# Decoder trunk on one core: weights and inputs of three TensorE stages put at other addresses, and the narrow score products of four head pairs reordered

## The chip, the core and the metric

The kernel runs on one core of a Trainium2 chip. The metric is the device time of one execution in microseconds (us); lower is better. The kernel before takes 551.02 us (median of three runs: 679.29, 551.02 and 550.89 us). A core has TensorE (PE in the profile; its weight loads are shown apart as PEld), VectorE (DVE), ScalarE (ACT), GpSimd (POOL) and SyncE (SP), which here issues nearly all DMAs. On-chip memory (SBUF) is addressed by a partition, of which there are 128, and a byte offset within it. When this text says that a tile lies "at 256", it means its byte offset within a partition modulo 512.

## The reference

One decoder layer for 256 tokens of width 1024: a convolution branch and a sparse-attention branch side by side, a cross-attention into 256 memory tokens, and a gated feed-forward block. Cut to what matters:

```python
h = rms_norm(x, norm_mix_g)
(u_conv, q, kc, vc, ks, vs, kw, vw, g_heads, g_conv, g_attn) = split(h @ w_in)
conv_out = conv_module(u_conv, ...)                  # gated, depthwise over time, layer norm, pointwise
nsa_out  = nsa_attention(q, kc, vc, ks, vs, kw, vw)  # compressed, selected and window branches
x = x + (sigmoid(g_conv) * conv_out + sigmoid(g_attn) * nsa_out) @ w_out

h = rms_norm(x, norm_x_g)
k, v = split(mem @ wkv)
s = einsum("bshd,bmhd->bhsm", h @ wq, k) / sqrt(256)
o = einsum("bhsm,bmhd->bshd", softmax(s), v)
x = x + o @ wo                                       # cross output

a, b = split(rms_norm(x, norm_ffn_g) @ ffn_in)
x = x + (silu(a) * b) @ ffn_out
return rms_norm(x, final_norm_g)
```

`ks` and `kw` are the keys of the selected and the window branch, `vs` and `vw` their values; 16 query heads share 4 groups of them. All arrays are float32. With 256 tokens, all four blocks of the selected branch are taken, so both branches see all earlier keys.

## The kernel before

**Products in three terms.** Each large product `W x` is formed from values split in two: a rounded copy (`..h`) and the remainder (`..l`). `split` (from L172) makes both for a half chunk of weights, 128 partitions by 4 blocks of 128 rows by 256 columns: ScalarE writes the copy (L184) and VectorE the remainder (L186). `rows` (L265 to L283) then issues three groups of 8 matmuls for a half chunk, each 128x128 by 256 columns: copy by copy, copy by remainder, remainder by copy. A chunk has two halves, so a chunk `ks`, `kw`, `gc0`, `xo0` and so on is 48 matmuls at L280. `x[..]` (the moving operand, or stream) and the weights each lie at one place modulo 512 throughout a group of 8. For `vs`, `vw` and the `v` chunks the roles are exchanged: the activations are loaded as weights and the weight tile is streamed.

**Where tiles lie.** The copies come from a ring `whi` of 5 buffers of 4096 bytes, the remainders from a ring `wlo` of 5. Large tiles share slots `L0` to `L14` and `LL` one after the other; a slot lies where its first tile was made, and it is as large as its largest tile. Added up in that order, L0 to L6, L9, LL, L10 and L14 start at 0 (modulo 512). L14 holds 8448 bytes, because of `kdl`, so L12, L11 and L13 start at 256. Behind L13 comes a filler tile `gap` of 320 bytes, and with it `whi` and `wlo` start at 64. So the usual pair is weights at 64, stream at 0 (`hh`, `hl`, `memh`, `meml`, `z`, `yh`, `yl`, `gh_1`, `gl_1` all lie at 0).

**Halves set apart.** `set_apart` (L195) puts one half chunk elsewhere: `k3_0` has its copy in L14 at 256 and its remainder in L10 at 448; `xq1_0` and `xo0_0` both have theirs in LL, at 256 and 448. The cross output's input `oxh` lies in L13, at 256, and `oxl` in L9, at 0 (L994). L11 holds `kvt`, then `sga`, then `pxh`; L13 holds `zins`, then `sgc`, then `oxh`; L14 holds, late in the program, `yl` and then `first_fo`, the first two half chunks of the feed-forward output weights, which are loaded long before use.

**Order.** The program is written as one sequence, and the framework's planner orders each engine's instructions when the program is built, by estimated times and the order in the text. On the chip each engine keeps that order and waits on semaphores. `in_line()` ties a matmul behind the one before it, so `ks` to `gc3`, the scores and the transposes stay in the written order on TensorE.

**Scores.** `scores(hp)` handles heads 2hp and 2hp+1 with queries in two halves. `later_half(hd)` is the second half of the queries against 512 key columns: two matmuls of 512 columns (L761, with `kdh` and then `kdl`). The first half of the queries needs 256 columns per head: two "narrow" matmuls each (L769). The order is wide (first head), narrow, narrow, wide (second head). VectorE then adds the bias and takes the minimum (L774 for the narrow results of both heads, then L780 for the wide ones). `scores(0)` stands before `ga3`, `scores(1)` in front of the second period, and so on through `between()`, which hands out the 8-matmul groups of `gc0` to `gc3` and `v0` to `v3` as filling.

**Cross output.** `cross_output(j)` (L1038) forms head j's output from `pxh`, `pxl` (both at 256) and `vxh`, `vxl` (both at 0, loaded as weights). `later_half(names, x)` below it runs `xo0` to `xo3` on `oxh`, `oxl`: the first halves of `xo0` to `xo2` fill in between the last softmax steps (L280), the second halves follow in one block of 72 matmuls (L1073), and `xo3` ends it with 48 (L280).

Of the kernel before, what the change touches and what calls it, by code (L numbers as in the profile page):

```python
# [10 lines left out]
F32R = mybir.dt.float32r  # L11
# [4 lines left out]
P = 128  # L16
D = 1024
S = 256
NB = D // P
# [79 lines left out]
def tile_hybrid_block(  # L99
# [15 lines left out]
    nc = tc.nc  # L115
    PSUM = bass.MemoryType.PSUM
    sb = ctx.enter_context(tc.tile_pool(name="sb", bufs=1))
# [4 lines left out]
    def long(name, slot, shape=(P, NB, S), dt=F32):  # L122

        return sb.tile(list(shape), dt, tag=f"L{slot}", name=name)

    def longs(names, slots, dt=F32R):
        return [long(n, i, dt=dt) for n, i in zip(names, slots)]
# [6 lines left out]
    def small(name, shape, dt=F32, tag=None, bufs=1):  # L134
        return sb.tile(shape, dt, tag=tag or name, name=name, bufs=bufs)

    def bank(name):

        four.append(0)
        if "s" in four[0] and len(four) % 2:  # L140
            return axp.tile([P, 2, S], F32, tag="s", name=name, bufs=2)
        return mmp.tile([P, 2, S], F32, tag="mm", name=name)
# [3 lines left out]
    def aux(name, shape, tag, bufs):  # L146
        return axp.tile(shape, F32, tag=tag, name=name, bufs=bufs)

    def f(ap):
        return ap.bitcast(F32)  # L150
# [20 lines left out]

    def split(w, shape, name):  # L172
        if name in apart:
            hi = apart[name]()[:, 64:].rearrange("p (k c) -> p k c", k=shape[1])
        else:
            hi = small(f"{name}h", shape, F32R, tag="whi", bufs=5)
        if name in apart:
            lo = aparts[name]().rearrange("p (k c) -> p k c", k=shape[1])
        else:
            lo = small(f"{name}l", shape, F32R, **places[1 - into_ffn(name)])  # L180

        n = 2 if name == "k1_0" else shape[1]
        with behind(*first.get(name, ())):
            copies = [nc.scalar.activation(hi[:, at:at + n], w[:, at:at + n], AF.Copy) for at in range(0, shape[1], n)]  # L184
            for at in range(0, shape[1], n):
                low = nc.vector.tensor_tensor(out=lo[:, at:at + n], in0=w[:, at:at + n], in1=f(hi[:, at:at + n]), op=ALU.subtract)  # L186
        splits[name] = copies[-1], low
        return hi, lo


    first, splits, apart = {}, {}, {}

    aparts = {}

    def set_apart(name, tag, low=None):  # L195

        pair = []

        def hi():
            pair.append(sb.tile([P, 1024 + 64 if low else 2 * 1024 + 112], F32R, tag=tag, name=f"{name}h"))  # L200
            return pair[0][:, 0:1024 + 64]

        def lo():
            if low:
                return sb.tile([P, 1024 + 112], F32R, tag=low, name=f"{name}l")[:, 112:]
            return pair[0][:, 1024 + 112:]

        apart[name], aparts[name] = hi, lo

    set_apart("k3_0", "L14", "L10")  # L210
    set_apart("xq1_0", "LL")
    set_apart("xo0_0", "LL")

    def behind(*marks):

        stack = ExitStack()
        for m in marks:
            stack.enter_context(tc.issue_after(m.ins))
        return stack
# [13 lines left out]
    def into_ffn(name):  # L233
        return name[0] == "f" and name[1] != "o"
# [9 lines left out]
    def halved(name, i):  # L244
        return split(raw(name, i), [P, 4, 256], f"{name}_{i}")
# [18 lines left out]
    last = []  # L264

    def in_line():
        return behind(*last)
# [17 lines left out]
    def sweep(*args, **kw):  # L285
        for _ in rows(*args, **kw):
            pass
# [94 lines left out]
    mem, h = (memh, meml), (hh, hl)  # L382
# [13 lines left out]
        ahead(name, slot)  # L396
    roots(0)

    small("gap", [P, 80])

    def kx(j):
        ps = gemm(f"k{j}", mem) if j else whole("k0", mem_t)
# [99 lines left out]
    with behind(loads["u6_1"]):  # L502
# [4 lines left out]
                     start=True, stop=True)  # L507
# [3 lines left out]
    for qb in range(2):  # L511
        for i, ns in enumerate(CGROUPS):
            n0, n1 = ns[0], ns[-1] + 1
            nc.tensor.matmul(cb_ps[:, qb, n0:n1].rearrange("p n h -> p (n h)"), lhsT=cbt[:, i, qb * P:qb * P + P],
                             rhs=relt[:, RT_CB + 16 * n0:RT_CB + 16 * n1], start=True, stop=True)
# [7 lines left out]
    def bias_of(hp):  # L523

        t = small(f"nb{hp}", [P, 2, S], tag="nb", bufs=2)
        for k in range(2):
            nc.sync.dma_start(t[:, k], bass.AP(tensor=row.tensor, offset=row.offset + 8 * 384 * (2 * hp + k) + P - 1,
                                               ap=[[384 - 16, 8], [-1, 16], [1, S]]))
        return t
# [180 lines left out]
    def qh(hd, qb):  # L710
        return qt[hd // 8][:, hd % 8, qb * P:qb * P + P]
# [34 lines left out]
    def heads_of(hp):  # L746
        return 2 * hp, 2 * hp + 1

    def scores(hp):

        g = hp // 2
        nbp = bias_of(hp)
        s0 = aux(f"s0_{hp}", [P, 2, 2, P], "s0", 1)
        p0 = small(f"p0_{hp}", [P, 2, 2, P], tag="p0", bufs=2)
        s1s, p1 = [], []

        def later_half(hd):
            s1 = aux(f"s1_{hd}", [P, 2, S], "s", 2)
            with in_line():
                for i, t in enumerate((kdh, kdl)):  # L760
                    mm = nc.tensor.matmul(s1, lhsT=qh(hd, 1), rhs=t[:, g].rearrange("p b t -> p (b t)"), start=i == 0, stop=i == 1)  # L761
            last[:] = [mm]
            s1s.append(s1)

        later_half(2 * hp)
        for k, hd in enumerate(heads_of(hp)):
            with in_line():
                for i, t in enumerate((kdh, kdl)):
                    mm = nc.tensor.matmul(s0[:, k], lhsT=qh(hd, 0), rhs=t[:, g, :, 0:P], start=i == 0, stop=i == 1)  # L769
        last[:] = [mm]  # L770
        later_half(2 * hp + 1)
        for k, hd in enumerate(heads_of(hp)):
            for br in range(2):
                red = nc.vector.tensor_tensor_reduce(out=p0[:, k, br], in0=s0[:, k, br], in1=nbp[:, k, P:S], scale=1.0, scalar=3e38,  # L774
                                                     op0=ALU.add, op1=ALU.min, accum_out=mins[:, hd, 0, br:br + 1])
        for k, hd in enumerate(heads_of(hp)):
            p1.append(small(f"p1_{hd}", [P, 2, S], tag="pr", bufs=4))
            for br in range(2):
                with behind(red):
                    low = nc.vector.tensor_tensor_reduce(out=p1[k][:, br], in0=s1s[k][:, br], in1=nbp[:, k], scale=1.0, scalar=3e38,  # L780
                                                   op0=ALU.add, op1=ALU.min, accum_out=mins[:, hd, 1, br:br + 1])
        mins_of.append(low)
        if hp == 1:
            first["gc2_1"] = red,
        return p0, p1
# [65 lines left out]

    mins_of = []
    p = [scores(0)]
    late = gate(3)
    with behind(mark):
# [28 lines left out]
    for hp, n in enumerate(PERIODS):  # L884
        if hp < 7:
            p.append(scores(hp + 1))
            with behind(*copies[-3:]):
                weights(hp + 1, *p[hp + 1])
        if hp == 2:
            pc_ps = aux("pc_ps", [P, 4, P], "pt", 2)  # L890
            with in_line():
                for qb in range(2):
                    for i in range(2):
                        mm = nc.tensor.transpose(pc_ps[:, 2 * i + qb], nsc[:, qb, 8 * i:8 * i + 8].rearrange("p h n -> p (h n)"), ident)
# [96 lines left out]

    r16 = rnorm(acc1, "2", 256.0)
    xmax, xneg, xsum = (small(n, [P, 4, 2]) for n in ("xmax", "xneg", "xsum"))
    oxh, oxl, pxh, pxl = longs(("oxh", "oxl", "pxh", "pxl"), (13, 9, 11, 12))  # L994
    queries = {}
    four[0] = ""

# [58 lines left out]
    def later_half(names, x):  # L1056

        pss = [bank(f"ps_{n}") if j < 2 else aux(f"ps_{n}", [P, 2, S], "s", 2) for j, n in enumerate(names)]
        parts = {}
        for n, ps in zip(names, pss):  # L1060
            for i in range(2):
                parts[n, i] = halved(n, i)
                if i == 0 or n == names[-1]:
                    with behind(*tail_mark) if n == names[0] else ExitStack():
                        sweep(ps, parts[n, i], x, i, line=False)
            if n == names[2]:
                for ks in ((0, 1), (2, 3)):
                    for m, qs in zip(names[:3], pss):
                        for row, (wi, xi) in enumerate(((0, 0), (0, 1), (1, 0))):
                            for b in range(2):  # L1070
                                cs = slice(b * P, b * P + P)
                                for k in ks:
                                    nc.tensor.matmul(qs[:, b], lhsT=parts[m, 1][wi][:, k, cs], rhs=x[xi][:, 4 + k], start=False,  # L1073
                                                     stop=k == 3 and row == 2 and b == 1)
                        if ks[1] == 3:
                            yield m, qs
        yield names[-1], pss[-1]
# [224 lines left out]
```

## Time and profile before

| | |
|---|---|
| runs | 679.29, 551.02, 550.89 us; median 551.02 |
| profiled execution | 551.26 us, of which the span from its first to its last instruction is 549.2 us |
| TensorE busy | 541.3 us (99%), 3886 matmuls |
| VectorE, ScalarE, GpSimd busy | 417.9 us (76%), 360.4 us (66%), 140.0 us (25%) |
| DMA queue that SP feeds | 95.86 MB, 52.3% of 16 engines' span |
| granted TensorE clock, mean | 0.999 |

A row of the chain of waits gives a start in us from the span's beginning, a length in us and what ran, with the number of instructions. A row of the timeline has the same first two columns, then engine, line, operation, output and inputs, the shape and the count. Matmuls overlap: the length of a timeline row includes the tail of its last matmul, so the distance of one row's start to the next one's start is the time that the group took from TensorE. Buffer and chunk numbers are left out of names, so `ks_0h` is the copy of a first half.

### The profile page before, as it was taken

What the parts mean: (1) busy time and instruction counts of PE and PEld (TensorE: products, weight loads), DVE (VectorE), ACT (ScalarE), POOL (GpSimd) and SP (SyncE); (2) the same over time, 40 slices, a digit from 0 to 9 for tenths busy, and PEclk for the clock granted to TensorE, in tenths of its full rate; (3) what the DMA queues carried; (4) which work ended last, traced back from release to release, by engine and by line L of the source; (5) the groups of instructions that cost most, each with busy time, mean ns of one, the idle gap of its engine ahead of it and who ended that gap; (6) DMA issues with size and microseconds to landing.
All of it is one profiled execution on the core that took longest, in us unless ns stands there. A gap on an engine that the chain in (4) does not pass through costs nothing.

```text
span 549.2 us, 10209 instructions
## 1 busy us (share of the span) xinstructions
PE 541.3 (99%) x3886; PEld 501.3 (91%) x3886; DVE 417.9 (76%) x781; ACT 360.4 (66%) x681; POOL 140.0 (25%) x125
## 2 busy tenths in 40 slices
PE   8999999999999999999999999999999999999995
PEld 7999998899999999889999999988888888888884
DVE  3888977999998998894868675559878787965531
ACT  4677667679956899689547674477565656463431
POOL 0005999999995001000004100310000000000001
PEclk9999999999999999999999999999999999999999
DMA  8939714456366445334556640466565555177611
GB/s 303 416 125 341 291 25 132 130 170 238 124 214 191 153 144 177 106 116 155 185 198 203 226 150 1 158 226 215 194 204 178 203 175 175 38 237 255 197 40 76
DMA packets 29297, 97.30 MB, mean 177 GB/s; under 512 B 3136, under 2 KB 5440, under 8 KB 28992
## 3 DMA queue, kind: packets, MB, share of 16 engines
q1 hardware_dynamic: 28816, 95.86, 52.3%
q10 hardware_dynamic: 432, 0.79, 0.4%
q8 instruction: 30, 0.49, 0.4%
q14 instruction: 19, 0.16, 0.1%
HBM read 95.39 MB, written 1.25 MB: 176 GB/s over the span
## 4 chain that ended last, share of the span: by engine, by line
PE 94%; DMA 2%; issue 1%; DVE 1%; ACT 1%; SPq 0%; POOLq 0%; POOL 0%; DVEq 0%
PE ps_f L1113 15%; PE fo L1141 10%; PE ps_u L280 8%; PE ps_f L1111 7%; PE ps_q L310 5%; PE ps_ga L280 4%; PE ps_v L280 4%; PE ps_gc L280 4%; PE ps_pw L280 4%; PE ps_xq L280 4%; PE ps_k L280 3%; PE ps_xo L280 3%; PE ps_wo L280 2%; PE ps_xo L1073 2%; PE s L761 1%
## 5 line engine op out<-in xcount | busy, mean ns | idle before, releaser
L466 POOL TENSOR_TENSOR yt<-yt,vw 128x512 f32<-128x512 f32 x61 | 97.0, 1592 | 51.0 <-ACT vw L464 47.4
L464 ACT ACTIVATE vw<-vt,ppt 128x256 f32<-128x256 f32 x102 | 44.3, 498 | 11.4 <-POOL yt L466 11.3
L1113 PE MATMUL ps_f<-g,f_0h 128*128 128x512 f32 x176 | 47.8, 394 | 0.1
L1113 PE MATMUL ps_f<-g,f_1h 128*128 128x512 f32 x176 | 47.6, 391 | 0.0
L1183 POOL TENSOR_SCALAR x<-x,rr 128x512 f32<-128x512 f32 x1 | 0.7, 699 | 176.4 <-DVE rr L1153 176.4
L450 DVE SCALAR_TENSOR_TENSOR yp<-vt,ppt,yp 128x256 f32<-128x256 f32 x108 | 44.1, 480 | 0.2
L186 DVE TENSOR_TENSOR f_0l<-f,f_0h 128x1024 fp32r<-128x1024 f32 x22 | 26.9, 1223 | 19.6 <-PE ps_f L1111 19.6
L1113 PEld LDWEIGHTS ps_f<-g,f_1h 128*128 128x128 f32 x176 | 32.7, 188 | 6.9
L184 ACT ACTIVATE f_1h<-f 128x1024 fp32r<-128x1024 f32 x22 | 23.3, 1060 | 23.2 <-PE ps_f L1113 20.0
L1113 PEld LDWEIGHTS ps_f<-g,f_0h 128*128 128x128 f32 x176 | 31.5, 189 | 5.6 <-DVE ab L1116 0.3
L795 ACT ACTIVATE p<-p,mins 128x128 f32<-128x128 f32 (+1 forms) x64 | 28.3, 445 | 6.7 <-DVE mins L774 6.6
L310 PE MATMUL ps_q<-hf,q 128*128 128x256 f32 x128 | 28.5, 381 | 0.0
L1111 PE MATMUL ps_f<-g,f_0l 128*128 128x256 f32 x176 | 28.1, 281 | 0.0
L1111 PE MATMUL ps_f<-g,f_1l 128*128 128x256 f32 x176 | 28.0, 281 | 0.0
L186 DVE TENSOR_TENSOR f_1l<-f,f_1h 128x1024 fp32r<-128x1024 f32 x22 | 26.8, 1218 | 0.6 <-ACT f_1h L184 0.6
L1111 PEld LDWEIGHTS ps_f<-g,f_0l 128*128 128x128 f32 x176 | 25.5, 188 | 1.8
L310 PEld LDWEIGHTS ps_q<-hf,q 128*128 128x128 f32 x128 | 24.1, 190 | 3.3
L184 ACT ACTIVATE f_0h<-f 128x1024 fp32r<-128x1024 f32 x22 | 23.0, 1046 | 1.8 <-DMA f<-in_wst_dram 1.8
L1111 PEld LDWEIGHTS ps_f<-g,f_1l 128*128 128x128 f32 x176 | 23.9, 189 | 0.0
L1115 ACT ACTIVATE ab<-ps_f 128x256 f32<-128x256 f32 x44 | 16.4, 376 | 6.8 <-PE ps_f L1111 6.8
L981 POOL COPY acc<-s_wo 128x256 f32<-128x256 f32 x1 | 1.1, 1122 | 72.1 <-ACT s_wo L974 72.1
L324 ACT ACTIVATE uh<-sl 128x256 fp32r<-128x256 f32 x22 | 9.2, 418 | 14.3 <-DVE sl L1120 14.3
(550 smaller groups left out, 1555.1 us busy)
## 6 DMA issues: line engine op xcount, KB each, us to landing
f<-in_wst_dram SPq DMA_DIRECT2D x44, 512.0 KB, 3.7
fo<-in_wfo_dram SPq DMA_DIRECT2D x20, 512.0 KB, 4.0
u<-in_wst_dram SPq DMA_DIRECT2D x14, 512.0 KB, 5.7
q<-in_wst_dram SPq DMA_DIRECT2D x8, 512.0 KB, 5.3
ga<-in_wst_dram SPq DMA_DIRECT2D x8, 512.0 KB, 3.7
gc<-in_wst_dram SPq DMA_DIRECT2D x8, 512.0 KB, 3.7
v<-in_wst_dram SPq DMA_DIRECT2D x8, 512.0 KB, 4.3
pw<-in_wst_dram SPq DMA_DIRECT2D x8, 512.0 KB, 5.0
```

The costliest lines, as they stand in the source:

```text
L184: copies = [nc.scalar.activation(hi[:, at:at + n], w[:, at:at + n], AF.Copy) for at in range(0, shape[1], n)]
L186: low = nc.vector.tensor_tensor(out=lo[:, at:at + n], in0=w[:, at:at + n], in1=f(hi[:, at:at + n]), op=ALU.subtract)
L280: mm = nc.tensor.matmul(ps[:, b], lhsT=lhsT, rhs=rhs, start=row + b + kb == 0, stop=kb == NB - 1 and row == 2 and b == 1)
L310: mm = nc.tensor.matmul(ps[:, b], lhsT=w[:, k, cs], rhs=x[:, kb], start=kb + b == 0, stop=kb == NB - 1 and b == 1)
L450: nc.vector.scalar_tensor_tensor(out=out[:, i] if t == ts[-1] else acc[i], in0=v, scalar=w, in1=acc[i], op0=ALU.mult, op1=ALU.add)
L464: nc.scalar.activation(pr[:, i], v, AF.Identity, scale=w, bias=col(PP_DB, j + i) if t == 0 else 0.0)
L466: nc.gpsimd.tensor_tensor(out=y, in0=y, in1=pr, op=ALU.add)
L795: exp.append(nc.scalar.activation(t, t, AF.Exp, scale=-1.0, bias=mins[:, hd, qb, br:br + 1], accum_out=sums[:, hd, qb, br:br + 1]))
L1111: nc.tensor.matmul(ps[:, 1], lhsT=w, rhs=fg(kb)[:, 0], start=False, stop=kb == NB - 1)
L1113: nc.tensor.matmul(ps, lhsT=w, rhs=fg(kb), start=kb == 0, stop=False)
L1115: nc.scalar.activation(ab[:, b], ps[:, 0], AF.Copy)
L1141: nc.tensor.matmul(accs[c][tb], lhsT=t, rhs=w[:, k], start=False, stop=kb == NF - 1 and t is tl)
```

## The change

Three edits.

First, `set_apart` gets a parameter `at`, and `ks_0`, the first half of `ks`, is set apart: its copy in L11 with no lead, which is at 256, and its remainder in L13 behind 48 floats, which is at 448. It no longer takes a buffer of `whi` and `wlo`. `k3_0` and `xq1_0` stay where they were.

Second, `xo0_0` is no longer set apart; it takes its buffers from `whi` and `wlo`, at 64. `oxh` gets 32 floats (128 bytes) of lead in L13, which puts it at 384. `oxl` goes from L9 into L14, with the same lead, which puts it at 128. L13 thereby grows by 128 bytes, and the filler `gap` shrinks by 128 bytes (80 to 48 floats), so that everything behind it stays where it was.

Third, in `scores` the two narrow matmuls of the second head are issued after that head's wide ones for hp 0 to 3. For hp 4 to 7 the order stays.

```diff
-            hi = apart[name]()[:, 64:].rearrange("p (k c) -> p k c", k=shape[1])
+            hi = apart[name]().rearrange("p (k c) -> p k c", k=shape[1])
...
-    def set_apart(name, tag, low=None):
+    def set_apart(name, tag, low=None, at=64):
...
-            pair.append(sb.tile([P, 1024 + 64 if low else 2 * 1024 + 112], F32R, tag=tag, name=f"{name}h"))
-            return pair[0][:, 0:1024 + 64]
+            pair.append(sb.tile([P, 1024 + at if low else 2 * 1024 + at + 48], F32R, tag=tag, name=f"{name}h"))
+            return pair[0][:, at:1024 + at]
...
-                return sb.tile([P, 1024 + 112], F32R, tag=low, name=f"{name}l")[:, 112:]
-            return pair[0][:, 1024 + 112:]
+                return sb.tile([P, 1024 + at + 48], F32R, tag=low, name=f"{name}l")[:, at + 48:]
+            return pair[0][:, 1024 + at + 48:]
...
     set_apart("k3_0", "L14", "L10")
+    set_apart("ks_0", "L11", "L13", 0)
     set_apart("xq1_0", "LL")
-    set_apart("xo0_0", "LL")
...
-    small("gap", [P, 80])
+    small("gap", [P, 48])
...
-        later_half(2 * hp)
-        for k, hd in enumerate(heads_of(hp)):
+        def first_half(k):
             with in_line():
                 for i, t in enumerate((kdh, kdl)):
-                    mm = nc.tensor.matmul(s0[:, k], lhsT=qh(hd, 0), rhs=t[:, g, :, 0:P], start=i == 0, stop=i == 1)
-        last[:] = [mm]
+                    mm = nc.tensor.matmul(s0[:, k], lhsT=qh(2 * hp + k, 0), rhs=t[:, g, :, 0:P], start=i == 0, stop=i == 1)
+            last[:] = [mm]
+
+        later_half(2 * hp)
+        first_half(0)
+        if hp >= 4:
+            first_half(1)
         later_half(2 * hp + 1)
+        if hp < 4:
+            first_half(1)
...
-    oxh, oxl, pxh, pxl = longs(("oxh", "oxl", "pxh", "pxl"), (13, 9, 11, 12))
+    pxh, pxl = longs(("pxh", "pxl"), (11, 12))
+    oxh, oxl = (long(n, i, (P, NB * S + 32), F32R)[:, 32:].rearrange("p (k s) -> p k s", k=NB) for n, i in (("oxh", 13), ("oxl", 14)))
```

## The prediction

> **What bounds the kernel now.** I read the page first, then TensorE's own waits, then the chain of waits in order of time.
>
> ```profile
> span 549.2 us, 10209 instructions
> ...
> PE 541.3 (99%) x3886; PEld 501.3 (91%) x3886; DVE 417.9 (76%) x781; ACT 360.4 (66%) x681; POOL 140.0 (25%) x125
> ...
> PE 94%; DMA 2%; issue 1%; DVE 1%; ACT 1%; SPq 0%; POOLq 0%; POOL 0%; DVEq 0%
> ```
>
> ```profile
> PE ps_k L310 <- DMA k0w<-in_wst_dram: 0.6, 1, 0.6
> PE ps_wo L280 <- DVE x L972: 0.3, 1, 0.3
> ```
>
> TensorE is busy for 541.3 of 549.2 us, and apart from the start its longest wait on anything is 0.3 us. So no wait is there to be removed. The end moves only if TensorE spends less time on the same matmuls. The change removes none, so what counts is the time of one matmul, stage by stage. The chain of waits gives it as a length over a count:
>
> ```profile
> 31.94 42.84 PE ps_u L280 x378
> 121.98 5.65 PE ps_ks L280 x48
> 138.95 5.65 PE ps_vw L280 x48
> 168.60 5.66 PE ps_ga L280 x48
> 174.26 5.65 PE ps_gc L280 x48
> 181.31 3.77 PE ps_gc L280 x32
> 189.61 4.72 PE ps_gc L280 x40
> 344.39 8.48 PE ps_xo L1073 x72
> 352.87 5.65 PE ps_xo L280 x48
> ```
>
> The same 256-column matmul with weights at 64 and stream at 0 takes 42.84 / 378 = 113.3 ns in the `u` stage and 5.65 / 48 = 117.7 ns in `ks` (8.48 / 72 = 117.8 in the cross output). I call these the fast and the slow regime; the gap is 4.4 ns. Since the addresses of `u` and `ks` are equal modulo 512, the regime is not set by the addresses alone: it is entered somewhere and then held for dozens of matmuls. Where it is entered, the timeline of TensorE shows around `k3_0`, the one half chunk of that stage that lies apart (copy at 256, remainder at 448):
>
> ```profile
> 25.55 1.12 PE L280 MATMUL ps_k<-memh,k_0h 128*128 128x256 f32 x8
> 26.51 1.12 PE L280 MATMUL ps_k<-meml,k_0h 128*128 128x256 f32 x8
> 27.47 1.07 PE L280 MATMUL ps_k<-memh,k_0l 128*128 128x256 f32 x8
> 28.38 1.07 PE L280 MATMUL ps_k<-memh,k_1h 128*128 128x256 f32 x8
> 29.28 1.07 PE L280 MATMUL ps_k<-meml,k_1h 128*128 128x256 f32 x8
> ```
>
> Distances of starts, over 8: 120 ns, 120, 114, 112.5 (rounded to 10 ns in the rows). With the weights at 256 and the stream at 0 a matmul takes 120; at 448 the fast 113 is there at once, and `k3_1` at 64 keeps it. The second place is the end of the cross output:
>
> ```profile
> 342.20 0.64 PE L1038 MATMUL xo_ps<-pxh,vxh 128*128 128x256 f32 x4
> 342.68 0.64 PE L1038 MATMUL xo_ps<-pxh,vxl 128*128 128x256 f32 x4
> ...
> 344.22 0.63 PE L1073 MATMUL ps_xo<-oxh,xo_1h 128*128 128x256 f32 x4
> 344.69 0.63 PE L1073 MATMUL ps_xo<-oxl,xo_1h 128*128 128x256 f32 x4
> ```
>
> Weights at 0 and stream at 256 again take 0.48 / 4 = 120 ns, but what follows, weights at 64 with streams at 256 and 0, is slow (0.47 / 4 = 117.5), and stays slow to the end of `xo3`. Taking place of weights minus place of stream, modulo 256: both 120 runs are at 0; after such a run a distance of 192 (448 - 0) gave the fast regime and a distance of 64 (64 - 256, 64 - 0) the slow one. I use this as a working rule; two places are thin support.
>
> **Part 1, `ks_0` at 256 and 448.** It repeats the order 120 run, 192, 64 in front of `ks_1`. Its own cost: 16 matmuls at 120 instead of 117.7 are +0.04 us, 8 at 113.3 are -0.04 us, so nothing. Behind it `ks_1` and `kw` are 72 matmuls at distance 64, and `vs`, `vw` another 96, weights at 0 and stream at 64, distance 192. If the fast regime holds up to the gate logits' product behind `vw`: 168 x 4.4 = 0.74 us gained; if it is lost where the roles are exchanged, 72 x 4.4 = 0.32; if it isn't entered, 0. That the exchanged places can run fast is shown by one group of `v1`, 1.82 / 16 = 113.8 ns:
>
> ```profile
> 227.51 1.82 PE ps_v L280 x16
> ```
>
> I take 0.74. The slots must be free in time: the last readers of L11 and L13 before are the first two rows here (the second is the timeline's group, with the first and the last start), and the split of `ks_0` starts later than both and waits on its DMA, not on a slot:
>
> ```profile
> 93.81 2.72 DVE L549 TENSOR_TENSOR zins<-kvt,ppt 128x960 f32<-128x960 f32 x1
> L568 PE MATMUL z_ps<-zins,w1t x64: 222/222/270, 97.9 to 100.6; 128*64 128x64 f32 x64
> 114.67 1.06 ACT L184 ACTIVATE ks_0h<-ks 128x1024 fp32r<-128x1024 f32 x1 [2.26 <-DMA ks<-in_wst_dram]
> ```
>
> So no new wait, and the later halves get a ring buffer sooner, which is hidden behind TensorE anyway.
>
> **Part 2, cross output.** `oxh` at 384 and `oxl` at 128 with weights at 64 are both at distance 192. After the 120 run of `cross_output(3)` the rule says fast: 72 + 48 = 120 matmuls x 4.4 = 0.53 us gained, or 0 if the regime stays slow. The 16 matmuls of `xo0_0`'s copy leave 256 for 64: 16 x (120 - 117.7 or 113.3) = 0.04 to 0.11 us gained; its 8 remainders may lose 0.04. I take 0.6 for the part. `xo0_0` now takes a ring buffer, so the sixth half, `xo2_1`, waits for its release around 338 instead of being split at 327; its first use is the third group of the block, at 347. ScalarE and VectorE together need about 2.3 us for a half, so it has 6 us to spare. What the move of `oxl` into L14 does to `first_fo` is the rival below.
>
> **Part 3, the narrow scores.** The first of the four affected groups:
>
> ```profile
> 167.05 0.40 PE L761 MATMUL s<-kdh,qt 128*128 128x512 f32 x1
> ...
> 167.52 0.28 PE L769 MATMUL s<-kdh,qt 128*128 128x256 f32 x1
> ...
> 168.44 1.10 PE L280 MATMUL ps_ga<-hh,ga_0h 128*128 128x256 f32 x8
> ```
>
> The group takes 1.39 us, and its eight matmuls stay. In another order they may each fall differently by a few ns: bounded by 4 to 13 ns a matmul as between 113 and 120 above, at most 8 x 7 ns x 4 groups = 0.2 us either way; I take 0. What matters is the regime behind them. `ga3`, `gc0`, 32 of `gc1` and 40 of `gc2` follow a group and are slow: 168 matmuls, 0.74 us if all turn fast, nothing to lose beyond 168 x (120 - 117.7) = 0.4 us. No row shows what a narrow matmul on `kdl` (at 256) before weights at 64 leads to. I give it an even chance and take 0 for the forecast. VectorE starts on the narrow results; the second head's now arrive some 0.46 us later (two wide matmuls), and VectorE, ScalarE and then the transposes are queued behind. The transposes of a pair stand a period behind its scores (what follows two successive groups starts at 181.31 and 189.61, 8.3 us apart), and TensorE waited for none of them, so this costs nothing; a pair that came 0.46 us too late four times would cost 1.8.
>
> **Sum.** Profiled 551.26 - 0.74 - 0.6 = 549.9; the median of the runs shown lies 0.24 lower, at 551.02, which gives 549.7. All the gain passes to the end, because the stages behind are TensorE-bound as well.
>
> **A rule that speaks against it.** The Trainium skill, page "SBUF — State Buffer", sections "SBUF: two separate sides" and "A bandwidth-pool intuition that's wrong", says that among the engines only the port pair shared by VectorE and GpSimd causes contention, that TensorE waits on nobody, and that weight loads have an independent read port. By that rule the places of weights and stream could not matter, and both address edits would give 0: 551.0 us, or 550.3 with part 3. The trace differs: 120 against 114 ns for the same shape, in the `k3_0` rows.
>
> **Rivals.** (1) Nothing flips, or addresses do nothing: 551.0. For it: the regime is held by history that I can't derive. Against it: the two places above. (2) All three parts flip: 549.7 - 0.74 = 548.9. (3) Only some: part 1 half or not at all, or part 2 not, with or without part 3, 549.5 to 550.5. (4) Slower, through `first_fo`:
>
> ```profile
> 300.05 0.33 SPq L252 DMA_DIRECT2D first_fo<-in_wfo_dram  x1
> first_fo<-in_wfo_dram SPq DMA_DIRECT2D x2, 512.0 KB
> 360.00:365.00 5.00, 5.00 (x28) 4.03 (x27) 3.01 (x5) 3.81 (x6) 0.95 (x2) 1.00 0.92 302
> 360.55 1.06 ACT L184 ACTIVATE f_1h<-f 128x1024 fp32r<-128x1024 f32 x1 [2.18 <-DMA f<-in_wst_dram]
> 362.85 0.71 PE L1113 MATMUL ps_f<-g,f_1h 128*128 128x512 f32 x2
> ```
>
> These two loads, 1 MB, go out at 300 while DMA has room. With `oxl` in L14 they can't start before `xo3` ends, at 358.5, which is where the first feed-forward weights come in with the DMA engines at 0.92 and 302 GB/s (the row of the windows). At that rate 1 MB is 3.5 us. The second chunk's last half is split at 360.55, straight after its DMA, and used at about 362.9, so it has about 1.2 us of slack. If the planner puts `first_fo` ahead of that half's load on SP, the load waits and is late by up to 3.5 us, 2.3 of them on TensorE. With the gains that is 549.7 + 2.3 = 552.0, and more if SP is held with several loads behind it. Against it: the planner would have to place them before loads that become ready 3 us earlier; behind those, the chunks from `f2` on have several us of slack, and it costs nothing. It decides by SP's order alone.
>
> **Chances.** Forecast (parts 1 and 2): 0.28. All three: 0.22. Some: 0.30. Nothing: 0.11. Slower by `first_fo` or another change of the planned order: 0.09. The range 548.4 to 551.6 takes in all but the last with a spread of about 0.4 us to either side. 2%, about what a measurement of this kernel can tell from no change, is 11 us, out of reach for any case: faster 0.01, within 0.98, slower 0.01.
>
> **What would show it.** In the chain of waits, `ks` to `vw` at 5.65 become about 5.44 for 48 (113.3 each); the L1073 block falls from 8.48 to 8.16 and `xo3` from 5.65 to 5.44; `ga3` and `gc0` show part 3 in the same way. `first_fo` will stand near or after 358. Wrong would be: blocks at 117.7 still (the rule fails), or a TensorE wait on DMA between 360 and 372 (rival 4).

## The result

The changed kernel takes 554.82 us (median of four runs, 554.44 to 555.09) against 551.16 us for the kernel before (median of four). The ratio is 1.0058, with a 95% interval of 1.0046 to 1.0070: slower by about 3.2 us (3.7 by these two medians), where 549.7 was forecast. It lies above the predicted range. The loss comes through `first_fo`, as in the prediction's rival 4, but at a higher price than that rival gave and without the condition that it named.

The page of the changed kernel, with the lines that answer to those of before:

```profile
span 552.9 us, 10209 instructions
...
PE 542.0 (98%) x3886; PEld 501.2 (91%) x3886; DVE 418.8 (76%) x781; ACT 359.5 (65%) x681; POOL 141.8 (26%) x125
...
PE 89%; DMA 4%; ACT 2%; DVE 2%; issue 2%; SPq 0%; POOLq 0%; POOL 0%; ACTq 0%; DVEq 0%
```

TensorE is about as busy as before (542.0 us instead of 541.3), but the span is 3.7 us longer and the chain runs over DMA, ScalarE and VectorE for 8% of it, where it was 4%. The chain of waits in order of time, for the stages that the edits touch:

```profile
32.04 42.84 PE ps_u L280 x378
122.08 5.54 PE ps_ks L280 x48
127.62 5.44 PE ps_kw L280 x48
138.50 5.44 PE ps_vw L280 x48
143.94 1.90 PE g_ps L637 x16
168.29 5.65 PE ps_ga L280 x48
173.94 5.65 PE ps_gc L280 x48
...
344.87 7.08 PE ps_xo L1080 x60
488.55 55.80 PE fo L1148 x246
```

Part 1 did what it was to do: `kw` to `vw` take 5.44 us for 48 matmuls, 113.3 ns each, instead of 5.65. Part 3 switched nothing: `ga3` and `gc0` are still at 5.65, and so are the 32 and 40 of `gc1` and `gc2`, at 3.77 and 4.72. Part 2 switched nothing either: 7.08 / 60 = 118 ns in the block. The same view of the kernel before shows how the difference of the two grows:

```profile
144.60 1.88 PE g_ps L637 x16
218.67 3.77 PE ps_v L280 x32
285.09 4.55 DMA xq<-in_wst_dram
295.20 5.73 PE ps_wo L280 x48
484.84 55.80 PE fo L1141 x246
```

The row at 218.67 stands in both views, word for word. The rows of the changed kernel that stand against the next two:

```profile
285.09 4.81 DMA xq<-in_wst_dram
295.46 5.92 PE ps_wo L280 x48
```

At 144 us the changed kernel is 0.66 us ahead (143.94 against 144.60). At 168.29 it is only 0.31 ahead (168.60 in the prediction's rows): at 151.55 TensorE's transposes of `sgn` (L693) had to wait for ScalarE. At 218.67 both kernels start the same 32 matmuls at the same time: the gain is gone, and the second half of it went with part 3, as experiment 4 shows. At 285.09 both issue the same load of `xq`; in this execution it takes 0.26 us longer, and TensorE goes on 0.26 us later. The 48 matmuls of `wo3` behind it then take 5.92 us instead of 5.73. The cross output's block starts 0.48 us later (344.87 against 344.39), and the last stage 3.71 us later (488.55 against 484.84). So 3.2 of the 3.7 us arise between the cross output and the last stage, in the feed-forward part.

TensorE's own waits in the changed kernel:

```profile
PE ps_f L1120 <- DVE g L984: 1.3, 1, 1.3
PE fo L1100 <- ACT rf L1090: 1.2, 1, 1.2
```

These two, 2.5 us, are new, and neither is a wait on DMA by name. SyncE's and ScalarE's timeline of the changed kernel show what is behind them:

```profile
350.55 6.70 SPq L241 DMA_DIRECT2D f<-in_wst_dram  x5
358.09 1.64 SPq L252 DMA_DIRECT2D first_fo<-in_wfo_dram  x2
359.81 19.01 SPq L241 DMA_DIRECT2D f<-in_wst_dram  x8
```

```profile
362.77 1.06 ACT L184 ACTIVATE f_1h<-f 128x1024 fp32r<-128x1024 f32 x1 [3.33 <-DMA f<-in_wst_dram]
364.98 1.06 ACT L184 ACTIVATE f_0h<-f 128x1024 fp32r<-128x1024 f32 x1 [1.15 <-DMA f<-in_wst_dram]
365.94 0.61 ACT L980 ACTIVATE s_xo<-x 128x512 f32<-128x512 f32 x1
368.76 1.06 ACT L184 ACTIVATE f_1h<-f 128x1024 fp32r<-128x1024 f32 x1 [1.41 <-DMA f<-in_wst_dram]
...
375.27 0.40 ACT L1090 ACTIVATE rf<-sp 128x256 f32<-128x256 f32 x1
```

`first_fo`'s two loads, at 300 before, are issued from 358.09 on, when the last matmul on `oxl` is done, and SP has them behind the fifth feed-forward half (`f2_0`) and ahead of the sixth (`f2_1`). ScalarE stands idle for 3.33 us until `f1_1`'s weights are there and 1.15 until those of `f2_0` are. Behind these two splits in its queue stands the residual of `xo3` (`s_xo`, then the gain), whose result `g` TensorE needs for the last two of the eight blocks of rows of every feed-forward product; it starts at 365.94. Further on, `rf` stands behind the splits of `f2_1` to `f4_0` and starts at 375.27. In the kernel before the same two stand at 363.21 and 371.87:

```profile
363.21 0.61 ACT L974 ACTIVATE s_xo<-x 128x512 f32<-128x512 f32 x1
...
371.87 0.40 ACT L1083 ACTIVATE rf<-sp 128x256 f32<-128x256 f32 x1
```

The order on TensorE has changed as well. The four `fo` matmuls that wait for `rf` came 20 matmuls behind the four of `sp`, from which `rf` is made, in the kernel before; in the changed kernel they come 7 matmuls behind. The first two rows are of before, the others of the changed kernel:

```profile
370.79 0.60 PE L371 MATMUL sp<-cpt,r 128*128 128x128 f32 x4
...
374.83 0.49 PE L1093 MATMUL fo<-cpt,x 128*128 128x128 f32 x3
```

```profile
373.09 0.60 PE L371 MATMUL sp<-cpt,r 128*128 128x128 f32 x4
...
375.72 0.66 PE L1100 MATMUL fo<-cpt,x 128*128 128x128 f32 x4 [1.20 <-ACT rf L1090]
```

The planner chose this order for the changed kernel; experiment 5 has it with nothing but the slot of `oxl` changed. The experiments that have the planned order of before in this part of TensorE (1, 2, 4, 6 and 10) show no wait for `rf`, and those that have the order of the changed kernel (3 and 5) show it.

A window of the changed kernel shows the load on the DMA engines in its last two columns (share and GB/s):

```profile
360.00:365.00 5.00, 4.71 (x26) 3.63 (x25) 2.68 (x3) 1.08 (x2) 0.00 (x0) 1.00 0.99 330
```

### The profile page after: what moved, and what is told of

Same layout as the page of the kernel before. It is cut to its first block, busy times and chain, and to the rows that moved or that the text cites. A ratio compares the mean times of both kernels' runs of the same rounds, so it can differ in the third digit from the quotient of the medians.

```text
span 552.9 us, 10209 instructions
## 1 busy us (share of the span) xinstructions
PE 542.0 (98%) x3886; PEld 501.2 (91%) x3886; DVE 418.8 (76%) x781; ACT 359.5 (65%) x681; POOL 141.8 (26%) x125
## 4 chain that ended last, share of the span: by engine, by line
PE 89%; DMA 4%; ACT 2%; DVE 2%; issue 2%; SPq 0%; POOLq 0%; POOL 0%; ACTq 0%; DVEq 0%
PE ps_f L1120 13%; PE fo L1148 10%; PE ps_u L280 8%; PE ps_f L1118 7%; PE ps_q L310 5%; PE ps_gc L280 4%; PE ps_v L280 4%; PE ps_pw L280 4%; PE ps_xq L280 4%; PE ps_ga L280 3%; PE ps_k L280 3%; PE ps_wo L280 2%; DMA f<-in_wst_dram 2%; PE ps_xo L280 2%; PE s L761 1%
```

## The experiments

Ratios are to the kernel before in runs on the same chip, with 95% intervals. Executions of one kernel differ by 1 to 4 us, in one group by 4.6 (the kernel before: 550.7 to 553.0 in the first group, 550.5 to 555.1 in the last), so a single trace shows where time goes, and the ratio shows how much.

**1. The changed kernel with `first_fo` in a free slot.** L9 has been free since `oxl` left it.

```diff
-    first_fo = long("first_fo", 14, (P, 4, 512))
+    first_fo = long("first_fo", 9, (P, 4, 512))
```

> The changed kernel with one edit: first_fo, the first two half chunks of the feed-forward output weights, lies in L9 (free since oxl left it) instead of L14, so its two loads can go out near 300 us again. Addresses of all matmul operands of the cross output, ks and the scores stay as in the changed kernel. Theory T, the transfer: the 3.7 us come from those two loads falling into the start of the feed-forward stage. Then the first feed-forward matmul still starts about 0.4 us later than before, but the three TensorE waits behind it (0.4, 1.5 and 1.4 us at 363 to 375 us) go, and the time is 551.3 to 551.8. Theory R, the regimes: the time comes from slower matmuls or from the order of the scores. Then it stays at 554.5 to 555.

Measured: 551.81 against 551.69, ratio 0.9997 (0.9986 to 1.0008). With the loads early again, no wait of TensorE in the feed-forward part is left, and the 3 us are gone. So the loss hangs on the slot of `first_fo`. The edit changes two things at once, though: the loads are early again, and the planner's order on ScalarE, VectorE and TensorE from 360 us on is that of before again. What is left of the three edits is no gain.

**2. `ks_0` alone.** The kernel before with part 1.

```diff
+    set_apart("ks_0", "L11", "L13", 0)
```

> The kernel before with part 1 alone: ks_0 set apart at 256 and 448. Theory A, absorbed: ks to vw take 5.54 and three times 5.44 us as in the changed kernel, 0.7 us less than before, but a later stage waits for ScalarE or VectorE at an anchor that has not moved, and the end stays at 550.8 to 551.3. Theory K, kept: TensorE is the bound throughout, and the time falls to 550.2 to 550.5.

Measured: 551.19 against 551.69, ratio 0.9987 (0.9978 to 0.9997): 0.7 us below by the ratio, 0.5 by the medians. That fits the gain of 0.74 reaching the end, though the interval runs from 0.2 to 1.2 us, and the trace has only 0.16 of it at the `ga3` row (168.44).

**3. The cross output alone.** The kernel before with part 2.

```diff
-    set_apart("xo0_0", "LL")
...
-    oxh, oxl, pxh, pxl = longs(("oxh", "oxl", "pxh", "pxl"), (13, 9, 11, 12))
+    pxh, pxl = longs(("pxh", "pxl"), (11, 12))
+    oxh, oxl = (long(n, i, (P, NB * S + 32), F32R)[:, 32:].rearrange("p (k s) -> p k s", k=NB) for n, i in (("oxh", 13), ("oxl", 14)))
```

> The kernel before with part 2 alone: oxh at 384, oxl in L14 at 128, xo0_0 in the ring. Theory T: first_fo goes out at about 358 us and the feed-forward start loses as in the changed kernel: 554.3 to 555.2. Theory R: the loss needs the scores' order or ks: 550.5 to 551.5.

Measured: 553.64, ratio 1.0035 (1.0021 to 1.0049). TensorE waits 1.3 us for `rf`, as in the changed kernel, and the block is still slow (8.48 us for 72). This part alone carries most of the loss, 1.9 of 3.2 us. The row of its waits:

```profile
PE fo L1093 <- ACT rf L1083: 1.3, 1, 1.3
```

**4. The scores alone.** The kernel before with part 3 (`first_half(1)` behind the second `later_half` for hp below 4).

> The kernel before with part 3 alone: the second head's narrow matmuls last for hp 0 to 3. ga3, gc0, 32 of gc1 and 40 of gc2 stay at 117.7 ns a matmul as in the changed kernel. Theory T: 550.8 to 551.4. Theory R, the order of the scores delays the softmax and with it later stages: 552 or more.

Measured: 552.32, ratio 1.0008 (0.9997 to 1.0018). No regime behind the scores changes (`ga3` and `gc0` at 5.65), and the order is worth nothing or costs a little. The trace shows where it costs: up to 190 us this execution runs 0.07 us behind the kernel before, and at the 32 matmuls that both kernels of the result start at 218.67 it is 0.38 behind:

```profile
219.05 3.77 PE ps_v L280 x32
```

So about 0.3 us go between 190 and 219 us: 0.1 in the 24 matmuls of `gc` at 199.86, which take 2.83 us instead of 2.73, and the rest behind 213, where the planner's order on TensorE differs from before, in this kernel and in the changed one alike.

**5. The late transfer without any address.** `oxl` in L14 lies at 0, as in L9, so only `first_fo`'s loads move.

```diff
-    oxh, oxl, pxh, pxl = longs(("oxh", "oxl", "pxh", "pxl"), (13, 9, 11, 12))
+    oxh, oxl, pxh, pxl = longs(("oxh", "oxl", "pxh", "pxl"), (13, 14, 11, 12))
```

> The kernel before with one edit: oxl goes from L9 into L14, at the same place modulo 512 (0), so that no address of a matmul's operands changes modulo 512 and first_fo has to wait for the end of xo3. Theory T (the whole loss is first_fo's two loads, which stand on SP behind f2_0's load and ahead of f2_1's): the f stage loses 3 to 3.7 us, the median is 3 to 3.7 above the kernel before, about 554.7 to 555.4 where before is 551.7; TensorE shows a wait of about 1.3 us for ScalarE's rf. Rival A (the late load costs only together with the moved addresses or the regrouped xo0_0): less than 1 us above before, under 552.7.

Measured: 553.91, ratio 1.0044 (1.0027 to 1.0060), with the waits of the changed kernel:

```profile
PE fo L1093 <- ACT rf L1083: 1.2, 1, 1.2
...
PE ps_f L1113 <- DVE g L978: 0.7, 1, 0.7
```

The slot alone costs 2.1 us by the medians (2.4 by the ratio). That is less than the 3 to 3.7 expected, but it shows that neither the moved addresses nor the regrouped `xo0_0` are needed for this much of the loss. Here too the planner's order differs from before, from 367 us on (30 places on TensorE, 3 on ScalarE, 4 on VectorE).

**6. `first_fo` late, but behind `f5_1`.** The changed kernel, L14 kept, the two loads queued later on SP.

```diff
-            his[k0], los[k0] = half(wfo[c, :, k0:k0 + 2], f"fo{c}_{k0}")
+            with behind(loads["f5_1"]) if c == 0 and k0 < 4 else ExitStack():
+                his[k0], los[k0] = half(wfo[c, :, k0:k0 + 2], f"fo{c}_{k0}")
```

> The changed kernel with first_fo's two loads issued behind the load of f5_1 instead of between f2_0 and f2_1; L14 is kept. Theory T with the prediction's own claim (it decides by SP's order alone, and behind the first chunks the loads cost nothing): f2_0 is split near 362.3 as before, no wait of TensorE over 0.5 us in the f stage, 551.8 as with first_fo in L9. Rival (the hole only moves): 1 MB is 3.5 us of the DMA engines wherever it stands, chunks f6 to f8 come late and TensorE waits for them, 553 to 555.

Measured: 551.14, ratio 0.9994 (0.9983 to 1.0005). The same bytes behind six chunks cost nothing; behind two and a half chunks they cost 3 us. As in experiment 1, the order on the other engines is that of before again. The profiled execution was the slowest of its ten (552.76; the others from 550.65) and shows that the place stays sensitive without `first_fo` too:

```profile
PE ps_f L1120 <- DVE g L984: 1.5, 1, 1.5
```

```profile
361.74 1.06 ACT L184 ACTIVATE f_1h<-f 128x1024 fp32r<-128x1024 f32 x1 [2.87 <-DMA f<-in_wst_dram]
```

The first row is one of its waits, the second of ScalarE's timeline: `f1_1`'s weights are nearly as late as in the changed kernel (3.33 us idle there), with `first_fo`'s loads 14 us away, at 375.96. So the wait for `g` alone doesn't show `first_fo` at work.

**7. The late loads kept, the queue changed.** The changed kernel with the splits of `f1_1`, `f2_0` and `f2_1` queued behind `xo3`'s residual on ScalarE and VectorE. `top` and `low` are the two instructions that write the gain's copy and remainder.

```diff
...
+                if n == "xo3" and b:
+                    first["f1_1"] = first["f2_0"] = first["f2_1"] = top, low
```

> The changed kernel, first_fo late as in it, with the splits of f1_1, f2_0 and f2_1 queued on ScalarE and VectorE behind xo3's residual. Theory Q (of the changed kernel's loss the part that stands behind g, 1.5 us, comes from the queue, the rest from late weights): the wait of 1.3 to 1.5 us for VectorE's g is gone, later waits for f2's and f3's halves remain; 1 to 2 us below the changed kernel, 553 to 554 where before is 551.7. Rival (TensorE only waits elsewhere for the same loads, the order gives nothing): 554.5 or more.

Measured: 552.40 against 551.78, ratio 1.0005 (0.9988 to 1.0022), where the changed kernel had 1.0058: 0.0053, or 2.9 us, come back although `first_fo` is as late and as large as before. ScalarE's timeline in this kernel:

```profile
361.29 0.63 ACT L980 ACTIVATE s_xo<-x 128x512 f32<-128x512 f32 x1 [2.73 <-DVE x L978]
...
366.03 1.06 ACT L184 ACTIVATE f_1h<-f 128x1024 fp32r<-128x1024 f32 x1 [1.42 <-DMA f<-in_wst_dram]
```

The residual starts at 361.29, 4.7 us sooner than in the changed kernel, and no wait for `g` or `rf` is left. I had expected 1 to 2 us, with the rest put down to late weights. So loads as late as these need not cost anything: the order of instructions decides. Which engine's order it is, this run doesn't separate, because the planner changed TensorE's with it (76 places from 364 us on). The `fo` matmuls now come 32 matmuls behind `sp`:

```profile
371.47 0.60 PE L371 MATMUL sp<-cpt,r 128*128 128x128 f32 x4
...
377.45 0.60 PE L1102 MATMUL fo<-cpt,x 128*128 128x128 f32 x4
```

One reserve: the profiled execution was among the faster ones (551.13 of 550.36 to 553.01), so the trace shows the mechanism, and the ratio its size.

**8. What steers the regime: `xo0_1` at 256 and 448.** The kernel before with `ks_0` apart, and `xo0_1` in place of `xo0_0` in LL. The cross output's inputs stay at 256 and 0.

```diff
-    set_apart("xo0_0", "LL")
+    set_apart("xo0_1", "LL")
```

> The kernel before with ks_0 set apart, and with xo0_1 set apart in LL (256 and 448) in place of xo0_0; the cross output's inputs stay at 256 and 0. Theory W (weights at 448 behind a run of 120 ns switch to the fast regime, wherever the stream lies): in the block of 72, 16 matmuls at 120 and 56 at 113.3, 8.27 us instead of 8.48, and xo3 5.44 instead of 5.65; xo0_0 no longer helps the first halves, about 40 matmuls lose 4.4 ns each (0.18). Net 0.25 below ks_0 alone: ratio about 0.998 to the kernel before. Theory D (the distance of weights and stream decides, 192 modulo 256 is fast): the same, since 448 - 256 and 448 - 0 are both 192. Theory H (the regime is held by something else, places do not steer it here): 8.48 and 5.65, and 0.1 to 0.2 above ks_0 alone.

Measured: 551.49, ratio 0.9994 (0.9984 to 1.0003). The regime switched as hoped. In the timeline `xo3`'s six groups of 8 start 0.91 apart, (357.10 - 352.56) / 40 = 113.5 ns a matmul:

```profile
352.56 1.07 PE L281 MATMUL ps_xo<-oxh,xo_0h 128*128 128x256 f32 x8
...
357.10 1.07 PE L281 MATMUL ps_xo<-oxh,xo_1l 128*128 128x256 f32 x8
```

The gain did not arrive, since the planner's order of ScalarE had changed with it: `f2_1`'s split now stands ahead of `xo3`'s residual,

```profile
363.41 1.06 ACT L184 ACTIVATE f_1h<-f 128x1024 fp32r<-128x1024 f32 x1 [0.78 <-DMA f<-in_wst_dram]
364.38 0.61 ACT L975 ACTIVATE s_xo<-x 128x512 f32<-128x512 f32 x1
```

and TensorE waits 1.2 us for `g`. This is one of the two waits of the changed kernel again, with `first_fo` early.

**9. The same half with the inputs at 384 and 128.** The first experiment's kernel with `set_apart("xo0_1", "LL")` added. Here weights at 448 are at distance 64 from both streams, which the prediction's rule calls slow.

> The changed kernel with first_fo in L9 (so that its loads are early) and with xo0_1 set apart in LL (256 and 448); the cross output's inputs stay at 384 and 128. Theory W: as in the kernel with inputs at 256 and 0, the block of 72 falls from 8.48 to between 8.15 and 8.3 and xo3 to 5.44; about 0.3 below the changed kernel with first_fo in L9 (551.8), 551.5. Theory D: 448 - 384 = 64 and 448 - 128 = 320, both 64 modulo 256: slow, 8.48 and 5.65, 551.8.

Measured: 551.26, ratio 0.9993 (0.9981 to 1.0005). `xo3` is fast all the same:

```profile
352.40 1.07 PE L281 MATMUL ps_xo<-oxh,xo_0h 128*128 128x256 f32 x8
...
356.93 1.07 PE L281 MATMUL ps_xo<-oxh,xo_1l 128*128 128x256 f32 x8
```

Five groups lie between these starts, (356.93 - 352.40) / 40 = 113.3 ns. So the distance from the stream does not decide, and theory D, the rule of the prediction, falls. The copy at 256 takes 120 ns here as well (starts 0.48 us apart for 4, at 344.13, 344.61 and 345.09), though its distance from these streams is 128. The place of the weights (theory W) fits so far.

**10. Both rings at 448.** The kernel before with a smaller filler ahead of the rings and 128 bytes behind them. Every engine's instructions stay in the same order, and only places change.

```diff
-    small("gap", [P, 80])
+    small("gap", [P, 48])
...
             lo = small(f"{name}l", shape, F32R, **places[1 - into_ffn(name)])
+            if not splits:
+                small("gap2", [P, 32])
```

> The kernel before with both rings of weight halves (whi and wlo) at 448 instead of 64: the filler gap shrinks from 320 to 192 bytes and a filler of 128 bytes behind the rings puts the rest back. Every engine's instructions stay in the same order, so only places change. Theory W (weights at 448 lead into the fast regime and hold it, whatever the stream's place): ga3, gc0, gc1, gc2 and the other blocks of weights at 117.7 ns turn to 113.3; the span has some 600 such matmuls before the feed-forward stage, 600 x 4.4 = 2.6 us, less where roles are exchanged (ks to vw) or where the first feed-forward loads become the limit; 1 to 2.6 us below the kernel before, ratio 0.995 to 0.998. Theory D (192 modulo 256 from the stream): weights at 448 with streams at 0 and 256 are at 192, the same. Rival H (a regime is only switched by a change of place, a uniform ring keeps whatever it had): the slow blocks stay slow, 551.7.

Measured: 556.05 against 551.84, ratio 1.0078 (1.0062 to 1.0094): slower by 4.2 us. The chain shows where:

```profile
32.36 44.52 PE ps_u L282 x378
...
489.26 57.18 PE fo L1143 x246
```

The `u` stage, fast in every kernel with the rings at 64, is slow: 44.52 / 378 = 117.8 ns. The two rows make 3.1 of the 4.2 us. Theory W falls too: weights at 448 do not by themselves lead into the fast regime. In the four places looked at where a half chunk apart switched the regime (`k3_0`, `ks_0`, and `xo0_1` with both pairs of inputs) the weights went from a ring at 64 to 256, then 448, and back to 64. With the ring at 448, `k3_0`'s 256 and 448 no longer switch it. What stands is theory H in this form: the regime is held, and that passage switches it. Why it does is not settled.

**11. Both rings at 448, with the queue changed** (as in experiment 7, for `f2_0` and `f2_1`, on the kernel of experiment 10).

> The kernel before with both rings at 448 and with the splits of f2_0 and f2_1 behind xo3's residual, as in the other kernel with that order. If theory W holds, TensorE reaches the feed-forward stage about 2 us sooner, and there the order on ScalarE counts: at least as fast as with the rings at 448 alone, by up to 1.2 us. If the loads are the limit there, the same as with the rings alone. If W fails, within 0.3 us of the kernel before.

Measured: 556.70, ratio 1.0087 (1.0071 to 1.0104). The slow `u` stage and last stage stay, and the order brings nothing here: 1.0078 and 1.0087 have intervals that overlap.

**12. `ks_0` and the queue.** The kernel before with part 1 and with `f2_0`'s and `f2_1`'s splits behind `xo3`'s residual.

> The kernel before with ks_0 set apart and with the splits of f2_0 and f2_1 behind xo3's residual; the cross output as before. Theory Q (the order counts only where TensorE reaches the feed-forward stage earlier than the queue on ScalarE): the gain of ks_0 alone, about 0.7, plus 0 to 0.4 for the waits that some executions have there: ratio 0.998 to 0.9987, so that xo0_1 is worth at least 0.4 of the 1.7 us by which the kernel with all three is below before. Rival (the order alone gives most of it): 0.9972 or less.

Measured: 550.77 against 551.78, ratio 0.9976 (0.9963 to 0.9989). This lies between the two forecasts and decides for neither.

**13. `ks_0`, `xo0_1` and the queue.** The kernel of experiment 8 with the same order.

> The kernel with ks_0 and xo0_1 set apart, and with the splits of f2_0 and f2_1 queued on ScalarE and VectorE behind xo3's residual (sum of squares and the two gains). Theory Q (that kernel lost its 0.42 us because ScalarE's queue had f2_1's split, which waits for its load, ahead of xo3's residual, and TensorE waited 1.2 us): the wait is gone, the gain of ks_0 and of xo0_1 arrives: 0.5 to 1.3 us below the kernel before, 0.9976 to 0.999. Rival: the loads themselves are the limit, f1_1 then shows the wait instead: no better than 0.9994.

Measured: 549.89 against 551.84, ratio 0.9969 (0.9955 to 0.9982), 1.7 us below: the fastest here, ahead of both kernels. After the start no wait of TensorE is listed, and the chain has the cross output at its new length:

```profile
343.67 8.27 PE ps_xo L1076 x72
351.93 5.44 PE ps_xo L281 x48
```

8.27 and 5.44 are the forecast of experiment 8 (16 matmuls at 120 and 56 at 113.3, then 48 at 113.3). Beside experiment 8 the order (TensorE's changed with it, in 30 places) is worth 0.0025, or 1.4 us; `xo0_1` is worth 0.4 us beside experiment 12, with intervals that overlap.

## Why the prediction was wrong

**"Behind those, the chunks from f2 on have several us of slack, and it costs nothing."** This is the step that failed, and with it rival 4's condition ("if the planner puts `first_fo` ahead of that half's load") and its chance of 0.09. SP had `first_fo` behind `f1_1`'s and `f2_0`'s loads, where it was said to be free, and it cost 3 us. The slack was taken from when TensorE needs the weights. But the splits are instructions on ScalarE and VectorE, which work through their queues in order, and a split that waits for its load also holds what is queued behind it. The half directly behind `first_fo` is `f2_1`: its split waits 1.41 to 1.61 us for its load in the traces of the changed kernel and of experiments 3 and 5, and not at all in the trace of before. `rf` stands behind it, and starts 2.2 to 2.3 us behind `sp` in these three, 1.08 in before (371.87 - 370.79). The Trainium skill, page "Perfetto Trace Analysis", section "Tensor Engine Instruction (MATMUL, LD_WEIGHTS)", calls ScalarE and VectorE strict FIFO. The rows agree: ScalarE is idle for 3.33 us up to 362.77, with `xo3`'s residual queued behind, whose input VectorE had written by 361.54.

**"It decides by SP's order alone."** This failed too. With the slot the planner changed the order on ScalarE, VectorE and TensorE. An estimate from the rows of the result: `rf` is written 2.58 us behind the start of `sp` in the changed kernel (375.27 + 0.40 - 373.09), and in before's order `fo` came 4.04 behind it (374.83 - 370.79); with that order TensorE would not have waited for `rf`. So this wait took both, a late `rf` and an early `fo`. Experiment 7 shows that another order brings back 2.9 us with the loads as late as before. No run has the late loads in the order of before, so how much of the 3 us each would cost alone stays open.

**"Against it: the planner would have to place them before loads that become ready 3 us earlier."** The planner didn't, and the loss came all the same. `f1_1`'s load was issued ahead of `first_fo`'s (it is the fourth of the five in the row at 350.55), and still its split began at 362.77 instead of 360.55. It is tempting to put this down to the 1 MB behind it, with the DMA engines busy to 0.99, but it isn't shown: in experiment 6 that split is at 361.74, without them. So the wait for `g` (1.3 us here, 0.7 in experiment 5, none in 3) can be scatter between executions in part or in whole.

**Part 1.** Mechanism and size were right: 0.74 forecast, 0.76 measured between the starts of `ks` and of the gate logits (144.60 - 121.98 against 143.94 - 122.08). Experiment 2 has 0.7 at the end, by the ratio.

**"All the gain passes to the end, because the stages behind are TensorE-bound as well."** For part 1 alone the time fits it (experiment 2); in the changed kernel it is wrong: half of the 0.66 us went by 152 to a wait for ScalarE, the rest by 218.67 with part 3, and the load of `xq` was issued at 285.09 in both traces. Experiment 8 shows the same further on, where an earlier TensorE ran into a queue that had not become earlier. A long share of busy time does not say that the next stage can start sooner.

**Part 2, the working rule.** It failed: -0.6 forecast, 0 measured in the block. Its two places had 448 for the weights as well as 192 for the distance, and the reading took the wrong one. Experiment 9 separates them, and experiment 10 shows that 448 is not enough either. The 120 run of `cross_output(3)` on which the rule built was there only in part in the changed kernel:

```profile
342.22 0.63 PE L1045 MATMUL xo_ps<-pxh,vxh 128*128 128x256 f32 x4
342.69 0.64 PE L1045 MATMUL xo_ps<-pxh,vxl 128*128 128x256 f32 x4
```

0.47 / 4 = 117.5 ns for the first two groups, with weights and stream at the same two places as before; the third, from 343.16, takes 0.48. So the 120, too, depends on what ran ahead.

**Part 3.** Taken as 0 with an even chance of 0.74; it gave 0 in regime. The order of the instructions, bounded at 0.2 us, cost about 0.3 by 219 us, not in the four groups but in what follows them (experiment 4).

**The rule that spoke against it.** Experiment 10 settles it: places alone, with no instruction moved on any engine, cost 0.78%. The Trainium skill, page "SBUF — State Buffer", section "SBUF: two separate sides", has TensorE waiting on nobody, by which places could not matter; here the measurement differs and decides.

**The sum.** In the profiled executions 549.9 was forecast and 554.97 came, 5.07 us more: 1.34 of gain that did not arrive, 0.48 that the cross output began late (the load of `xq` and the slower `wo3`), and 3.23 in the feed-forward part, which add up to it within 0.02.

## What to carry to other kernels

When a change moves a transfer into a busy stretch, look at the queues of the engines that prepare its neighbours' data: an instruction that waits for a load holds everything behind it, so the slack to count is that of the next instruction in the queue, not that of the weights. Where a planner orders the instructions, compare its order on every engine before and after: moving one tile moved the order on three of them here. Work that needs no transfer belongs ahead of work that does, and it is cheap to say so in the order. A rule read from two places of a trace should be tested where its explanations differ before it is priced.

## What the runs showed of the hardware

The 256-column matmul runs at 113.3 or at 117.7 ns for long stretches, with the same addresses modulo 512 and the same instructions, and keeps its regime for hundreds of matmuls (378 in `u`). With the weight rings at 64, a half chunk at 256 and 448 switched it to 113.3 in each of the four places looked at; with the rings at 448 the same passage did not, and the kernel lost 4.2 us. Neither the places nor the instructions fix the regime: it can change across a pause of TensorE. Ahead of the pause before `wo3`, 0.6 to 1.5 us from start to start, the matmuls run at 113.3 ns in all fifteen traces; behind it, the last 32 of `wo3` run at 113.3 or 113.4 in eight of them and at 117.8 in seven. Experiments 2 and 12 have the same instructions up to there, in the same order and at the same places, and differ in this (5.62 us in experiment 2, at 294.75):

```profile
294.72 5.92 PE ps_wo L281 x48
```

What decides it wasn't studied. Loads at the start of the feed-forward part differ between executions: in the same two traces, with the loads issued in the same order, ScalarE waits 0.81 and 2.62 us for the weights of `f1_1`. That this scatter is what makes executions of one kernel differ by 1 to 4 us is likely from experiment 6, but it wasn't tested.
